# Norm chains without GpSimd, and a layer's modulation by TensorE instead of VectorE

## The chip, the cores and the metric

The kernel runs on one core of a Trainium2 chip. A core has five engines with queues of their own: TensorE (PE, matrix products), VectorE (DVE, elementwise work on two operands), ScalarE (ACT, functions and copies), GpSimd (POOL, elementwise work) and SyncE (SP, which here issues the DMAs). Each engine works through its queue in order and waits at semaphores for the others. The metric is the device time of one execution, in microseconds; smaller is better.

## The reference

A residual stream `x` of 512 tokens by 1024 features, and a context `xc` of 256 tokens, go through two blocks in fp32.

The first block has two layers. In each, a vector `c` gives six modulation vectors (shift, scale and gate for the mixer, and the same for the MLP), and `c_ctx` gives six for the context:

```python
sh1, sc1, g1, sh2, sc2, g2 = modulation(c, w_mod[l], b_mod[l])        # silu(c) @ w_mod + b_mod
csh1, csc1, cg1, csh2, csc2, cg2 = modulation(c_ctx, w_mod[l], b_mod[l])
px = modulate(rms_norm(x, norm1_g[l]), sh1, sc1) @ w_in[l]            # h * (1 + scale) + shift
...                                                                   # latent attention, Fourier mix, long convolution
x = x + g1 * heads_out(att_x, px, hy, w_out[l])
x = x + g2 * sq_relu_mlp(modulate(rms_norm(x, norm2_g[l]), sh2, sc2), w_mlp1[l], w_mlp2[l])
...                                                                   # in the first layer, the same for xc
```

A last `rms_norm` ends the block. The second block has two layers as well, with a norm on each sublayer's output too:

```python
u = rms_norm_2(h, norm_g[layer, 0]) * (1.0 + sc1) + sh1
y = hgrn2_mixer(u, ...)                      # layer 0; layer 1: dilated_attention_mixer
h = h + (1.0 + g1) * rms_norm_2(y, norm_g[layer, 1])
u = rms_norm_2(h, norm_g[layer, 2]) * (1.0 + sc2) + sh2
y = swiglu_ffn(u, ffn_w_in[layer], ffn_w_out[layer])
h = h + (1.0 + g2) * rms_norm_2(y, norm_g[layer, 3])
```

`rms_norm` divides by the root of the mean square over the 1024 features.

## The kernel before

Features lie on partitions: `x` is eight tiles of 128 features by 512 tokens. fp32 products are made of three products of split operands: every operand has a high part (a rounded cast by ACT) and a low part (the rest, one subtraction of two SBUF tiles). `mm3` (L153 to L155) issues high x high, high x low and low x high.

**Weights.** `wchunk` fetches a chunk of 128x1024 by a DMA from SP into `wr` (three buffers); ACT casts it to `w_h` (L118), and POOL subtracts to make `w_l` (L119). In some stretches there is a second ring of five buffers, `wx_h` and `wx_l` (`extra_ring`), so that the first eight chunks of a product (its head) are resident while two halves of the tokens pass. `gemm` goes over the chunks `m`; with `parts` the head is gone through once for each half of the tokens, so that the second half's norm runs beside the first half's products.

**Norms.** A norm over features is a chain. ACT squares a tile and DVE (or POOL, for the second half) adds it to the sum (`stat_add`, L284; `st_h` for 256 tokens, `st_f` for 512). A product with a matrix of ones (L307) sums over partitions; ACT and DVE make the reciprocal root `st_rh` (L316, L317). Then each tile is scaled (`md_h`, L326), and split into `u_h` and `u_l` (`modulate`, L335, L336): every third tile goes a second way, where ACT works twice and POOL subtracts (L333). In the second block a sublayer's output `y` is normed first: DVE makes `r_t` (L1292), adds it to `x` (L1293) and the squares of the new `x` are added for the next norm. `final_norm` (L1266) does the like between the blocks. These chains stand in a list, `self.chain`; `gemm` calls `link` after each chunk, which issues up to three steps of it. So they run beside the products of the other half.

The four places where the output of one part is normed, added and normed again are: the first block's end and the HGRN2 layer's start, that layer's output projection and its FFN's start, that FFN's end and the dilated attention's start, and that layer's output projection and its FFN's start.

**Modulation vectors.** They are products of one row with a large matrix. `mod_tasks` makes them on DVE: a piece of weights 128x512 (256 KB) comes into `mo_w`, and DVE multiplies it by a column of `c` and adds it to `mo_a` (L378 for the first of eight pieces, L380 for the others; for the first layer a second time with `c_ctx`). After eight pieces PE transposes `mo_a` (L363), and DVE reduces it over the 128 partial sums. The pieces are tasks in a list, `self.bgq`; `gemm` calls `bg(3)` after each chunk in w_in and w_out, which issues three of them. `run_late` puts the last step of a set behind the next chunk's products.

A scheduler then places each engine's instructions in its queue, by its own estimate of when their inputs are ready; so the order in a queue is not the order of the code.

Of the kernel before, what the change touches and what calls it, by code (L numbers as in the profile page):

```python
# [14 lines left out]
ALU = mybir.AluOpType  # L15
# [3 lines left out]
P = 128  # L19
D = 1024  # L20
KD = D // P
# [58 lines left out]
class Kern:  # L80
# [60 lines left out]
    def wchunk(self, src, n=1024, parts=P, extra=False, lo_eng=None):  # L141

        nc = self.nc
        raw = self.t(self.ring, [P, 1024], "wr", 3)
        nc.sync.dma_start(raw[:parts, :n], src)
        w = self.hl(self.xring, [P, 1024], "wx", 5) if extra else self.hl(self.ring, [P, 1024], "w", 3)
        w = w[:parts, :n]
        self.split(w, raw[:parts, :n], lo_eng or nc.gpsimd)
        return w
# [21 lines left out]
    def gemm(self, srcs, nk, rhs, segs, evac, head=2, parts=None, after=None, n=1024, bg=0, lead=2, dep=False):  # L171
# [11 lines left out]
        parts = [(x,) for x in parts] if parts else [seg(0)]  # L183
        short = self.xring is None and parts[-1][-1][1] - parts[-1][0][0] <= C
        load = lambda m, short=False: self.wchunk(
            srcs[m], n, extra=self.xring is not None and m > 2, lo_eng=self.nc.vector if short and m % 3 == 2 else None)
        head = min(head, len(srcs))
        keep = [load(m) for m in range(head)] if self.xring is not None else None
        for part in parts if head else ():
# [30 lines left out]
    @contextmanager  # L220
    def extra_ring(self, side="right"):
        with self.pool("xring", side) as p:
            self.xring = p
            yield
            self.xring = None
# [121 lines left out]
    def mod_tasks(self, pool, wkey, bcol, pairs, js, pad=0):  # L347
# [6 lines left out]
        for j in js:  # L354
            use = [pr for pr in pairs if j in pr[2]]
            for half in range(2):
# [29 lines left out]
                for k in range(KD):  # L386
                    tasks.append(lambda k=k, f=piece: f(k))
                tasks += [lambda: None] * pad
        return tasks

# [445 lines left out]
    def block1_layer(self, l):  # L836
# [56 lines left out]
        if not last:  # L893
            fl, self.bgq = self.bgq, self.mod_tasks(
                hvp, "w_mod0", self.bmod[0],
                [(self.c1, self.m1[0], range(2, 6)), (self.cc, self.mc[0], range(2, 6))], range(2, 4), pad=1)
            for i, step in enumerate(fl):
                self.bgq.insert(3 * i + 3 * (i > 0), step)
            win(0, 8, tok, evac_hyena, parts=SEGS)
            wes.close()  # L900
            mid = lay.enter_context(self.pool("mid"))
# [117 lines left out]
        if not last:  # L1019
# [9 lines left out]
            for k in range(4):  # L1029
# [3 lines left out]
            p = tmp.enter_context(self.pool("mods", "right"))  # L1033
            self.bgq += self.mod_tasks(
                p, "w_mod0", self.bmod[0],
                [(self.c1, self.m1[0], range(4, 5)), (self.cc, self.mc[0], range(4, 5))], range(4, 5), pad=1)

# [75 lines left out]
    def norm_to(self, pool, key, st, g, m, j, s, e, lag=0):  # L1113
# [7 lines left out]
        def tile(k):  # L1121
            o = j * KD + k
            self.modulate(pool, self.xk(k, s, e), v["r"], v["g"][:, k : k + 1], m[:, o : o + 1], self.u[k][:, s:e],
                          k % 3 == 2)

# [129 lines left out]
    def final_norm(self, s, e):  # L1255
# [8 lines left out]
        def tile(k):  # L1264
            x = self.xk(k, s, e)
            nc.vector.scalar_tensor_tensor(x, x, self.fin_g[:, k : k + 1], v["r"], op0=ALU.mult, op1=ALU.mult)  # L1266
            self.stat_add(self.stp, self.st[s], x, nc.gpsimd if s else None)

# [6 lines left out]
    def resid2(self, l, j, p, y, sty, s, e):  # L1275
# [13 lines left out]
        def tile(k):  # L1289
# [4 lines left out]
            if not last:  # L1294
                self.stat_add(self.stp, self.st[s], x, nc.gpsimd if s else None)
            elif k % 2:
# [23 lines left out]
    def hgrn(self, es_x):  # L1320
# [7 lines left out]
        with ExitStack() as es:  # L1328
# [9 lines left out]

            ws = [[self.wchunk(a["hg_wv"][c, kp], extra=4 * c + kp > 2) for kp in range(4)] for c in range(2)]
            for s, e in HALVES:  # L1340
# [200 lines left out]
    def dilated(self, es_x):  # L1541
        with ExitStack() as es:
            cp = es.enter_context(self.pool("cat"))
            cat = [self.hl(cp, [P, L], f"cat{k}") for k in range(KD)]
            with ExitStack() as hs:
                p = hs.enter_context(self.pool("qk"))
                self.dilated_heads(p, hs, es_x, cat)
            es_x.enter_context(self.extra_ring())
            with self.pool("y") as yp:
# [458 lines left out]
```

## Time and profile before

| | |
|---|---|
| median of 3 runs | 3566.88 us (3566.8 to 3569.93) |
| profiled execution | 3567.03 us |
| its span | 3565.2 us |
| PE busy | 3305.0 us, 93% |
| DVE busy | 2122.9 us, 60% |
| ACT busy | 1296.0 us, 36% |
| POOL busy | 1378.7 us, 39% |
| mean granted clock of PE | 0.969 |

The span runs from the first instruction to the last. An engine's busy time is that in which it executes; what it waited for is told by the table of waits, which names the engine, tile and line that released it. PE's granted clock is a share of full speed. Since only one engine is near its limit over the whole span, the stretches have to be looked at one by one.

### The profile page before, as it was taken

Reading aid. Unit: us, or ns where it says so; the run is one execution under the profiler, and the core shown is the slowest. Engines: PE = TensorE matmul, PEld = TensorE weight load, DVE = VectorE, ACT = ScalarE, POOL = GpSimd, SP = SyncE. Lnnn points to the kernel's source line nnn. Section 1 sums busy time; section 2 is a strip of 40 time slices with the busy share of each in tenths; the row PEclk is TensorE's granted clock in tenths of the full one; section 3 lists DMA queues with packets and bytes.
Section 4 is the critical chain, followed back from the end, with each engine's and each line's share of the span. In section 5 each row is a group of like instructions: output and inputs, shape, how many; then the busy total and the mean of one; then the engine's idle time right before and its main releaser. Section 6 shows DMA issues by size and latency. Waiting matters only on the chain. (4 is left out here: it accounts for less than half of the span.)

```text
span 3565.2 us, 46665 instructions
## 1 busy us (share of the span) xinstructions
PE 3305.0 (93%) x18232; PEld 2779.7 (78%) x18232; DVE 2122.9 (60%) x3144; ACT 1296.0 (36%) x2278; POOL 1378.7 (39%) x730
## 2 busy tenths in 40 slices
PE   7988988999998988999989898999899999989998
PEld 3776667888886766988877787888788878888887
DVE  7677778575466467757674656476585474461224
ACT  4235634121124346422245555222323323352222
POOL 2424434232234344434443344344433333434443
PEclk9989999999999999999999999999999999989999
DMA  6330044343343210345531123455313223322332
GB/s 207 122 98 26 24 136 122 119 123 122 122 127 95 95 45 30 110 136 188 184 122 57 56 85 93 150 183 186 101 52 101 92 75 100 102 65 89 95 95 71
DMA packets 145344, 374.31 MB, mean 105 GB/s; under 512 B 19515, under 2 KB 28770, under 8 KB 145124
## 3 DMA queue, kind: packets, MB, share of 16 engines
q1 hardware_dynamic: 140900, 367.14, 32.6%
q10 hardware_dynamic: 4224, 4.19, 0.3%
q8 instruction: 143, 2.34, 0.3%
q14 instruction: 77, 0.63, 0.1%
HBM read 364.98 MB, written 6.29 MB: 104 GB/s over the span
## 5 line engine op out<-in xcount | busy, mean ns | idle before, releaser
L119 POOL TENSOR_TENSOR w_l<-wr,w_h 128x1024 fp32r<-128x1024 f32 (+1 forms) x401 | 967.4, 2414 | 1642.5 <-ACT w_h L118 1592.6
L153 PE MATMUL A<-u_h,w_h 128*128 128x512 f32 (+1 forms) x2344 | 879.2, 376 | 12.8 <-ACT w_h L118 3.7
L154 PE MATMUL A<-u_l,w_h 128*128 128x512 f32 (+1 forms) x2344 | 874.9, 373 | 8.0 <-DVE u_l L336 5.5
L155 PE MATMUL A<-u_h,w_l 128*128 128x512 f32 (+1 forms) x2344 | 873.6, 373 | 8.3 <-POOL w_l L119 8.3
L118 ACT CAST w_h<-wr 128x1024 fp32r<-128x1024 f32 (+1 forms) x406 | 420.3, 1037 | 1085.2 <-PE A L154 725.9
L153 PEld LDWEIGHTS A<-u_h,w_h 128*128 128x128 f32 x2344 | 450.3, 192 | 103.4 <-ACT w_h L118 5.8
L155 PEld LDWEIGHTS A<-u_h,w_l 128*128 128x128 f32 x2344 | 450.9, 192 | 91.9 <-POOL w_l L119 10.0
L154 PEld LDWEIGHTS A<-u_l,w_h 128*128 128x128 f32 x2344 | 450.6, 192 | 91.1 <-DVE u_l L336 6.7
L380 DVE SCALAR_TENSOR_TENSOR mo_a<-mo_w,mc_c,mo_a 128x512 f32<-128x512 f32 x308 | 323.4, 1050 | 105.2 <-DMA mo_w<-in_ada_dram 59.4
L155 PE MATMUL A<-hid_h,w_l 128*128 128x512 f32 (+1 forms) x1072 | 376.9, 352 | 8.4 <-POOL w_l L119 8.4
L154 PE MATMUL A<-hid_l,w_h 128*128 128x512 f32 (+1 forms) x1072 | 378.6, 353 | 3.5 <-DVE hid_l L119 3.5
L153 PE MATMUL A<-hid_h,w_h 128*128 128x512 f32 (+1 forms) x1072 | 379.2, 354 | 1.9 <-ACT hid_h L118 1.9
L155 PEld LDWEIGHTS A<-hid_h,w_l 128*128 128x128 f32 x1072 | 203.4, 190 | 38.4 <-POOL w_l L119 10.5
L154 PEld LDWEIGHTS A<-hid_l,w_h 128*128 128x128 f32 x1072 | 203.8, 190 | 31.5 <-DVE hid_l L119 4.7
L153 PEld LDWEIGHTS A<-hid_h,w_h 128*128 128x128 f32 x1072 | 203.5, 190 | 30.1 <-ACT hid_h L118 2.9
L1751 DVE TENSOR_TENSOR sg<-A,sg 128x512 f32<-128x512 f32 (+1 forms) x52 | 31.4, 608 | 242.6 <-PE A L155 209.0
L119 POOL TENSOR_TENSOR wx_l<-wr,wx_h 128x1024 fp32r<-128x1024 f32 x55 | 134.4, 2457 | 79.4 <-ACT wx_h L118 74.7
L1134 DVE SCALAR_TENSOR_TENSOR x<-A,m,x 128x512 f32<-128x512 f32 (+1 forms) x96 | 62.0, 657 | 169.7 <-PE A L155 169.7
L284 DVE TENSOR_TENSOR st_h<-st_h,st_sh 128x256 f32<-128x256 f32 x137 | 108.6, 800 | 56.6 <-ACT st_sh L283 52.6
L1081 DVE TENSOR_TENSOR relu<-relu 128x512 f32<-128x512 f32 (+1 forms) x104 | 83.7, 833 | 82.5 <-ACT relu L1080 82.3
L1583 DVE TENSOR_TENSOR qk<-A,cos 128x512 f32<-128x512 f32 (+1 forms) x56 | 47.0, 841 | 131.0 <-PE A L155 130.8
L153 PE MATMUL A<-w_h,u_h 128*128 128x256 f32 (+1 forms) x408 | 120.7, 296 | 2.1 <-DVE rt L1586 2.1
(553 smaller groups left out, 6264.4 us busy)
## 6 DMA issues: line engine op xcount, KB each, us to landing
wr<-in_w_mlp_dram SPq DMA_DIRECT2D x139, 512.0 KB, 3.7
mo_w<-in_ada_dram SPq DMA_DIRECT2D x192, 256.0 KB, 3.5
wr<-in_ff_win_dram SPq DMA_DIRECT2D x88, 512.0 KB, 3.6
mo_w<-in_w_mod_dram SPq DMA_DIRECT2D x160, 256.0 KB, 3.1
wr<-in_at_wqk_dram SPq DMA_DIRECT2D x48, 512.0 KB, 3.6
wr<-in_ff_wout_dram SPq DMA_DIRECT2D x32, 512.0 KB, 3.6
wr<-in_w_in_dram SPq DMA_DIRECT2D x30, 512.0 KB, 3.6
wr<-in_w_out_dram SPq DMA_DIRECT2D x24, 512.0 KB, 3.6
```

Of the source, the lines that this page charges most:

```text
L118: nc.scalar.copy(dst.hi, src)
L119: (lo_eng or nc.vector).tensor_tensor(dst.lo, src, dst.hi.bitcast(F32), op=ALU.subtract)
L153: ins = mm(out, lhs.hi, rhs.hi, start=first, stop=False)
L154: mm(out, lhs.hi, rhs.lo, start=False, stop=False)
L155: mm(out, lhs.lo, rhs.hi, start=False, stop=last)
L284: (eng or nc.vector).tensor_tensor(acc, acc, sq, op=ALU.add)
L380: nc.vector.scalar_tensor_tensor(state[i], raw, cc[:, k : k + 1], state[i], op0=ALU.mult, op1=ALU.add)
L1081: nc.vector.tensor_tensor(r, r, r, op=ALU.mult)
L1134: nc.vector.scalar_tensor_tensor(x, ps, mod[:, o : o + 1], x, op0=ALU.mult, op1=ALU.add)
L1583: nc.vector.tensor_tensor(d, vw(ps), vw(c), op=ALU.mult)
L1751: nc.vector.tensor_tensor(sgs[s], ps, sgs[s], op=ALU.mult)
```

## The change

Five things change.

1. The low halves of weights in products that wait for a norm (`dep`: the first eight chunks or fewer of the MLPs, of the dilated attention's q and k, and of the FFNs), and those of the HGRN2 layer's first eight chunks, are made by DVE instead of POOL: 46 subtractions of 128x1024. Where there is a second ring, its chunks 3, 4 and 5 are loaded first.
2. The second ring has six buffers instead of five after the dilated attention.
3. `modulate` no longer sends every third tile of a norm over POOL; DVE makes all `u_l`.
4. The adds of squares of the second half in `final_norm` and `resid2` move from POOL to DVE: 28 of 128x256.
5. For the first layer, the mixer's gate and the MLP's shift and scale (for `c` and for `c_ctx`) are made by `mod_products` instead of `mod_tasks`. In twelve quarters of 256 outputs each, one DMA brings 128x8x256 weights (1 MB, a single buffer), and eight fp32 products use them as the moving operand; the stationary one, `c32`, has 32 columns, of which `c` and `c_ctx` are the first two and the rest zero. The eight products go to four column groups of PE, two after each other on each. ACT copies the 128x256 result out of PSUM, PE transposes it (two transposes), and DVE adds up the four groups. A quarter is five tasks: the load, three empty ones, the products.

```diff
         load = lambda m, short=False: self.wchunk(
-            srcs[m], n, extra=self.xring is not None and m > 2, lo_eng=self.nc.vector if short and m % 3 == 2 else None)
+            srcs[m], n, extra=self.xring is not None and m > 2,
+            lo_eng=self.nc.vector if dep or short and m % 3 == 2 else None)
         head = min(head, len(srcs))
-        keep = [load(m) for m in range(head)] if self.xring is not None else None
+        keep = None
+        if self.xring is not None:
+
+            order = sorted(range(head), key=lambda m: (m not in (3, 4, 5), m)) if dep else range(head)
+            keep = {m: load(m) for m in order}
...
+    def mod_products(self, pool, wkey, bcol, pairs, js, gap, rows_in):
...
+        c32 = self.t(pool, [P, KD, 32], "mp_c")
+        nc.gpsimd.memset(c32, 0.0)
+        nc.gpsimd.tensor_copy(c32[:, :, 0], self.c1)
+        nc.gpsimd.tensor_copy(c32[:, :, 1], self.cc)
+        for j in js:
+            for quarter in range(4):
+                state = {}
+
+                def load(j=j, quarter=quarter, state=state):
+                    self.run_late()
+                    half, c = divmod(quarter, 2)
+                    state["w"] = raw = self.t(pool, [P, KD, 256], "mp_w")
+                    nc.sync.dma_start(raw, self.a[wkey][j * 2 + half].rearrange("k p n -> p k n")[:, :, c * 256 : c * 256 + 256])
+
+                def products(j=j, quarter=quarter, state=state):
+                    ps = self.psa()[:, :256]
+                    for k in range(KD):
+                        g = 32 * (k % 4)
+                        nc.tensor.matmul(ps[g : g + 32], c32[:, k], state["w"][:, k], start=k < 4, stop=k >= 4,
+                                         tile_position=(0, g))
+                    state["a"] = self.t(rows_in[0], [P, 512], rows_in[1])[:, :256]
+                    nc.scalar.copy(state["a"], ps)
+                    self.late.append(lambda: finish(j * KD + quarter * 2, state["a"]))
+
+                def finish(o, rows):
+                    ps = self.psa()[:, :256]
+                    for m in range(2):
+                        nc.tensor.transpose(ps[:, m * P : (m + 1) * P], rows[:, m * P : (m + 1) * P], self.ident)
+                    sums = ps.rearrange("p (m g c) -> p m g c", g=4, c=32)
+                    for i, out in enumerate(pairs):
+                        nc.vector.reduce_sum(out[:, o : o + 2], sums[:, :, :, i], axis=AX.X)
+                        nc.vector.tensor_tensor(out[:, o : o + 2], out[:, o : o + 2], bcol[:, o : o + 2], op=ALU.add)
+
+                tasks += [load] + [lambda: None] * gap + [products]
+        return tasks
...
-            fl, self.bgq = self.bgq, self.mod_tasks(
-                hvp, "w_mod0", self.bmod[0],
-                [(self.c1, self.m1[0], range(2, 6)), (self.cc, self.mc[0], range(2, 6))], range(2, 4), pad=1)
+            fl, self.bgq = self.bgq, self.mod_products(hvp, "w_mod0", self.bmod[0], (self.m1[0], self.mc[0]), range(2, 4), 3,
+                                                    (hvp, "mp_a"))
...
-            self.bgq += self.mod_tasks(
-                p, "w_mod0", self.bmod[0],
-                [(self.c1, self.m1[0], range(4, 5)), (self.cc, self.mc[0], range(4, 5))], range(4, 5), pad=1)
+            self.bgq += self.mod_products(p, "w_mod0", self.bmod[0], (self.m1[0], self.mc[0]), range(4, 5), 3,
+                                          (self.stp, "st_r"))
...
-            self.modulate(pool, self.xk(k, s, e), v["r"], v["g"][:, k : k + 1], m[:, o : o + 1], self.u[k][:, s:e],
-                          k % 3 == 2)
+            self.modulate(pool, self.xk(k, s, e), v["r"], v["g"][:, k : k + 1], m[:, o : o + 1], self.u[k][:, s:e])
...
-            self.stat_add(self.stp, self.st[s], x, nc.gpsimd if s else None)
+            self.stat_add(self.stp, self.st[s], x)
...
-                self.stat_add(self.stp, self.st[s], x, nc.gpsimd if s else None)
+                self.stat_add(self.stp, self.st[s], x)
...
-            ws = [[self.wchunk(a["hg_wv"][c, kp], extra=4 * c + kp > 2) for kp in range(4)] for c in range(2)]
+            ws = [[self.wchunk(a["hg_wv"][c, kp], extra=4 * c + kp > 2, lo_eng=nc.vector) for kp in range(4)] for c in range(2)]
...
-            es_x.enter_context(self.extra_ring())
+            es_x.enter_context(self.extra_ring(6))
```

In the new file the lines named above stand seven lower, those from 1134 on 48 lower (L284 is L291, L1292 is L1340).

On DVE, after the HGRN2 layer's output projection, the order before, from the last steps of the first half's residual to that half's reciprocal root (`st_rh_18254`):

```order
L1292 SCALAR_TENSOR_TENSOR r_t_18188<-y_17769,gain_3407_18087,st_rh_18080 128x256
L284 TENSOR_TENSOR st_h_18089<-st_h_18089,st_sh_18179 128x256
L1293 TENSOR_TENSOR x_3881<-x_3881,r_t_18188 128x256
L284 TENSOR_TENSOR st_h_18089<-st_h_18089,st_sh_18185 128x256
L284 TENSOR_TENSOR st_h_18089<-st_h_18089,st_sh_18191 128x256
L284 TENSOR_TENSOR st_h_18074<-st_h_18074,st_sh_18220 128x256
L284 TENSOR_TENSOR st_h_18074<-st_h_18074,st_sh_18249 128x256
L316 SCALAR_TENSOR_TENSOR st_sh_18257<-B_18252,st_sh_18257 128x256
L284 TENSOR_TENSOR st_h_18074<-st_h_18074,st_sh_18297 128x256
L317 SCALAR_TENSOR_TENSOR st_rh_18254<-st_sh_18257,st_rh_18254 128x256
```

The same place after (the reciprocal root is `st_rh_18198`; L119 with `w_l` or `wx_l` is a subtraction that makes low halves of weights):

```order
L1341 TENSOR_TENSOR x_3853<-x_3853,r_t_18132 128x256
L119 TENSOR_TENSOR wx_l_18394<-wr_18391,wx_h_18393 128x1024
L291 TENSOR_TENSOR st_h_18033<-st_h_18033,st_sh_18129 128x256
L119 TENSOR_TENSOR wx_l_18400<-wr_18397,wx_h_18399 128x1024
L291 TENSOR_TENSOR st_h_18033<-st_h_18033,st_sh_18135 128x256
L291 TENSOR_TENSOR st_h_18018<-st_h_18018,st_sh_18164 128x256
L291 TENSOR_TENSOR st_h_18018<-st_h_18018,st_sh_18193 128x256
L119 TENSOR_TENSOR wx_l_18406<-wr_18403,wx_h_18405 128x1024
L119 TENSOR_TENSOR w_l_18412<-wr_18409,w_h_18411 128x1024
L323 SCALAR_TENSOR_TENSOR st_sh_18201<-B_18196,st_sh_18201 128x256
L291 TENSOR_TENSOR st_h_18018<-st_h_18018,st_sh_18241 128x256
L324 SCALAR_TENSOR_TENSOR st_rh_18198<-st_sh_18201,st_rh_18198 128x256
```

Four weight subtractions have come to stand between the residual and the reciprocal root; before, all eight were in POOL's queue.

On PE, at the end of the first layer's w_in, the order before (L966 and L967 double the rows of a key tile `kk`, L363 transposes `mo_a`, L548 belongs to the convolution):

```order
L966 MATMUL A_1814<-kk_h_1810,dupr_1283 128x512
L967 MATMUL A_1814<-kk_l_1811,dupr_1283 128x512
L966 MATMUL A_1824<-kk_h_1820,dupr_1283 128x256
L363 MATMUL A_1836<-c_ident_67,mo_a_342_1634 128x128 x4
L967 MATMUL A_1824<-kk_l_1821,dupr_1283 128x256
L363 MATMUL A_1843<-c_ident_67,mo_a_343_1636 128x128 x4
L548 MATMUL A_1897<-c_ident_67,eo_400_1890 128x128 x4
```

The same place after (L424 are the products on column groups, whose weights `mp_w` are the moving operand, L433 the transposes of their copied results `mp_a`):

```order
L1016 MATMUL A_1770<-kk_h_1766,dupr_1267 128x512
L1017 MATMUL A_1770<-kk_l_1767,dupr_1267 128x512
L1016 MATMUL A_1780<-kk_h_1776,dupr_1267 128x256
L424 MATMUL A_1784<-mp_w_1706,mp_c_485 32x256 x2
L1017 MATMUL A_1780<-kk_l_1777,dupr_1267 128x256
L424 MATMUL A_1784<-mp_w_1706,mp_c_485 32x256 x6
L433 MATMUL A_1795<-c_ident_67,mp_a_1793 128x128 x2
L424 MATMUL A_1804<-mp_w_1802,mp_c_485 32x256 x8
L433 MATMUL A_1815<-c_ident_67,mp_a_1813 128x128 x2
L599 MATMUL A_1869<-c_ident_67,eo_385_1862 128x128 x4
```

Two quarters of products stand here one behind the other, each with its transposes right behind it, where two sets of transposes of `mo_a` were.

## Rows read from the trace of the kernel before

**Rows 1.** The page: busy us, share of the span, instructions of each engine.

```profile
PE 3305.0 (93%) x18232; PEld 2779.7 (78%) x18232; DVE 2122.9 (60%) x3144; ACT 1296.0 (36%) x2278; POOL 1378.7 (39%) x730
```

**Rows 2.** PE's waits, whole span: us in total, times, longest.

```profile
PE B L307 <- DVE st_h L284: 46.6, 9, 8.4
PE A L155 <- POOL w_l L119: 22.1, 14, 2.6
PE B L307 <- POOL st_h L284: 13.7, 3, 5.5
PE B L307 <- DVE st_f L284: 12.3, 5, 4.3
PE A L363 <- DVE mo_a L380: 11.6, 1, 11.6
...
PE A L966 <- ACT kk_h L118: 6.8, 4, 2.3
```

**Rows 3.** Stretches: us long, busy us of PE, PEld, DVE, ACT, POOL, clock, DMA share.

```profile
485.00:498.00 13.00, 1.36 (x7) 0.94 (x6) 10.69 (x12) 2.86 (x4) 4.68 (x2) 0.71 0.75 234
1833.00:1891.00 58.00, 46.19 (x255) 40.38 (x254) 45.62 (x68) 29.24 (x56) 27.48 (x17) 0.82 0.29 87
2146.00:2201.00 55.00, 39.05 (x281) 37.18 (x280) 41.39 (x67) 28.87 (x63) 27.36 (x17) 0.90 0.30 89
2171.00:2176.00 5.00, 5.00 (x24) 4.83 (x23) 2.96 (x6) 1.74 (x5) 2.38 (x1) 0.50 0.50 116
2558.00:2607.00 49.00, 33.02 (x228) 31.81 (x227) 45.64 (x77) 21.09 (x45) 24.28 (x17) 0.82 0.30 92
3137.00:3185.00 48.00, 33.63 (x241) 32.48 (x240) 39.59 (x64) 24.37 (x55) 25.06 (x16) 0.84 0.30 88
```

**Rows 4.** Timeline of DVE: start us, us, operation, count.

```profile
2152.41 3.02 DVE L1292 SCALAR_TENSOR_TENSOR r_t<-y,gain,st_rh 128x256 f32<-128x256 f32 x2
2155.35 2.94 DVE L1293 TENSOR_TENSOR x<-x,r_t 128x256 f32<-128x256 f32 x2
2158.22 0.87 DVE L1292 SCALAR_TENSOR_TENSOR r_t<-y,gain,st_rh 128x256 f32<-128x256 f32 x2
2159.01 0.74 DVE L1293 TENSOR_TENSOR x<-x,r_t 128x256 f32<-128x256 f32 x2
```

**Rows 5.** Timeline of POOL from 2146.

```profile
2152.47 5.21 POOL L119 TENSOR_TENSOR w_l<-wr,w_h 128x1024 fp32r<-128x1024 f32 x2 [1.91 <-ACT w_h L118]
```

**Rows 6.** Groups of DVE, 2146 to 2201: count, busy us, mean ns, idle before.

```profile
L1292 DVE SCALAR_TENSOR_TENSOR r_t<-y,gain,st_rh 128x256 f32<-128x256 f32 x16 | 12.8, 835 | 0.1
L1293 DVE TENSOR_TENSOR x<-x,r_t 128x256 f32<-128x256 f32 x16 | 9.3, 618 | 0.0
L284 DVE TENSOR_TENSOR st_h<-st_h,st_sh 128x256 f32<-128x256 f32 x14 | 8.1, 600 | 0.7 <-ACT st_sh L283 0.6
L336 DVE SCALAR_TENSOR_TENSOR u_l<-md_h,m,u_h 128x256 fp32r<-128x256 f32 x6 | 6.5, 1104 | 3.0 <-ACT u_h L335 2.9
```

**Rows 7.** Groups of POOL, 2146 to 2201.

```profile
L284 POOL TENSOR_TENSOR st_h<-st_h,st_sh 128x256 f32<-128x256 f32 x7 | 6.1, 868 | 6.7 <-ACT st_sh L283 6.4
```

**Rows 8.** DVE on the tile w_l: min, median, max ns, first and last start.

```profile
L119 DVE TENSOR_TENSOR w_l<-wr,w_h x5: 1208/1212/2594, 527.2 to 1112.7; 128x1024 fp32r<-128x1024 f32 x5
```

**Rows 9.** Timeline of all engines, end of the first layer's mixer.

```profile
492.67 2.40 DVE L284 TENSOR_TENSOR st_f<-st_f,st_sq 128x512 f32<-128x512 f32 x1 [0.74 <-ACT st_sq L283]
...
497.11 1.97 PE L363 MATMUL A<-c_ident,mo_a 128*128 128x128 f32 x8 [11.64 <-DVE mo_a L380]
```

**Rows 10.** Timeline of PE, three places.

```profile
40.31 5.50 PE L822 MATMUL B<-wr,c 128*2 128x512 f32 x12
...
212.91 1.04 PE L363 MATMUL A<-c_ident,mo_a 128*128 128x128 f32 x8
...
1952.11 2.37 PE L1452 MATMUL A<-st,qd 128*32 128x128 f32 x32
```

**Rows 11.** The page, DMA issues: count, KB each, median us to landing.

```profile
wr<-in_w_mlp_dram SPq DMA_DIRECT2D x139, 512.0 KB, 3.7
```

More of the change, by code (lines that the diff above doesn't have):

```diff
@@ L145, in wchunk @@
         nc.sync.dma_start(raw[:parts, :n], src)
-        w = self.hl(self.xring, [P, 1024], "wx", 5) if extra else self.hl(self.ring, [P, 1024], "w", 3)
+        w = self.hl(self.xring, [P, 1024], "wx", self.xbufs) if extra else self.hl(self.ring, [P, 1024], "w", 3)
         w = w[:parts, :n]
@@ L220, in extra_ring @@
     @contextmanager
-    def extra_ring(self, side="right"):
+    def extra_ring(self, bufs=5, side="right"):
+        self.xbufs = bufs
         with self.pool("xring", side) as p:
@@ L388, in mod_tasks @@
                 tasks += [lambda: None] * pad
+        return tasks
+    def mod_products(self, pool, wkey, bcol, pairs, js, gap, rows_in):
+        nc = self.nc
+        tasks = []
+        c32 = self.t(pool, [P, KD, 32], "mp_c")
[28 more added lines that the diff above has]
+                tasks += [load] + [lambda: None] * gap + [products]
         return tasks
```

## The prediction

> **What bounds the kernel now.** I read the engine table first: TensorE (PE) is busy for 93% of the span [rows 1], so time can come only from its gaps, its clock, or its work. The table of PE's waits over the whole span is next [rows 2]. Its largest rows are not weights that arrive late but norms: the ones-matmul that sums squares (L307) waits for adds of squares, 46.6 us for VectorE (DVE) adds, 13.7 for GpSimd (POOL) adds, 12.3 for the 512-wide adds of the first block. One wait of 11.6 us is for the modulation sums (mo_a) that DVE makes, and 22.1 us in 14 waits are for low halves of weights that POOL makes.
>
> Third, the table of stretches [rows 3] shows where the norm waits lie: four places in which one sublayer's output is normed, added and normed again (1833 to 1891, 2146 to 2201, 2558 to 2607, 3137 to 3185). There DVE is busy for 41.4 of 55 us, 45.6 of 49, 39.6 of 48 and 45.6 of 58, and PE's granted clock is 0.82 to 0.90. DVE with its chain, not PE, sets the end of these stretches.
>
> Fourth, DVE's timeline at 2152 shows why [rows 4]: two r_t operations of 128x256 take 3.02 us, two adds to x 2.94; three microseconds later the same pairs take 0.87 and 0.74. In the first pair's time POOL runs two weight splits (L119), 5.21 us without a break [rows 5]. The stretched operations read two SBUF tiles each. So an operation of DVE with two SBUF inputs loses up to 1.5 us when it meets a POOL split.
>
> **The norm chains.** Take 2146 to 2201. The grouped rows [rows 6] give r_t 12.8 us (16), x 9.3 (16), the adds 8.1 (14), u_l 6.5 (6): 36.7 us. At the undisturbed pace of rows 4 (0.44 for r_t and, as the same kind, u_l; 0.37 for x and, as the same kind and size, the adds) they would take 16 x 0.44 + 16 x 0.37 + 14 x 0.37 + 6 x 0.44 = 20.7. So 16.0 us of DVE's time there are collisions. What comes to DVE in exchange: eight splits at 1.21, the median of the five that DVE makes today [rows 8], 9.7 us; POOL's seven adds, now 0.868 us each [rows 7], 7 x 0.37 = 2.6; two u_l, 0.9. Together 13.2. DVE's load falls by only 2.8 us.
>
> The gain is larger than that only if the splits fit where DVE sits idle, 55 - 41.4 = 13.6 us, most of it while a statistic goes through PE and ScalarE (ACT). DVE's new order puts four of the eight splits ahead of the first half's rstd, where it waits for adds and the statistic, three among that half's u tiles, and the last behind the second half's rstd, ahead of its r_t. If half of the 9.7 us falls into idle time, the stretch ends 2.8 + 4.9 = 7.7 us earlier; with all in it 12.5, with none of it 2.8, and if each split also holds up a link of the chain (eight times 1.21, nothing hidden) the stretch loses up to 7. I take 7, since the tail also loses POOL's slower adds. The stretch at 3137 has 8.4 us of idle time and the same operations: 7. The one at 2558 has only 3.4 us idle: 5. The one at 1833 has 12.4 but its chain also waits for PE's results on their way to x: 6. Together -25, and between +28 (four times 7) and -42 (12.5, 12.5, 2.8 + 8.4 and 2.8 + 3.4).
>
> By the Trainium skill, "SBUF — State Buffer", section "Who interferes with whom", a DVE instruction with two SBUF inputs contends with a GpSimd instruction that reads SBUF, and the loser is blocked for the other's whole length. The trace agrees (0.44 against 1.5 us each). By that rule a split on DVE is itself such an instruction, and would be blocked wherever POOL still works; the five of today reach from 1.21 to 2.59 us [rows 8], and at the far end eight would cost 11 us more in a stretch.
>
> **The other splits and tiles.** Fourteen more splits go to DVE, six at the first layer's MLP and eight at the second's. A share of the 22.1 us of waits for w_l [rows 2] lies at the end of the first layer's mixer and the start of its MLP; I take 4 us of gain there, 1 at the second layer, and 2 for the u_l tiles that no longer go over ACT twice and POOL. Sum -7; between +5 (DVE has no free time there either) and -14. The sixth buffer and the order in which head chunks are loaded I cost at nothing: transfers of 512 KB land in 3.7 us [rows 11], and the DMA share of those stretches is 0.29 to 0.30 [rows 3].
>
> **The modulation of the first layer.** Removed: 96 DVE operations, which costs PE nothing except where it waited. It did at 485: mo_a was late by 11.64 us, with an add of 2.40 us in its chain that met POOL [rows 9]. The 8.4 us wait of rows 2 ends at 2170; from 2171 to 2176 the granted clock was 0.50, 1.2 instead of 2.4 GHz [rows 3], which is 2.5 us of work lost; I take the same here. Of the 12.3 us of waits for 512-wide adds [rows 2], which share DVE's queue with such sums, I take 4. Gain 11.6 + 2.5 + 4 = 18.
>
> Added, all on PE: twelve quarters of eight products with 32x256 results. No row shows this shape. Sixteen fp32 matmuls of 32x128 on four column groups take 2.37 us (32 records, two each) [rows 10], 0.148 each: by number of matmuls a quarter costs 1.2 us, by columns 2.4. Plain fp32 on 512 columns costs 5.50 / 12 = 0.46 a record, two records each [rows 10], so 0.46 for 256 columns and 3.7 a quarter. Twelve quarters: 14, 28 or 44 us. I take 21, between the two readings of the nearest row, as that row can't tell overhead from columns. The transposes fall from six sets of eight at 1.04 us [rows 10] to twelve pairs, 6.2 to 3.1 us: -3.
>
> By the Trainium skill, "TensorEngine Tiling (Array Packing)", section "When to Use Tiling", a free dimension of 32 gives four-fold column tiling. With that the plain price would fall to 11 us, and the sum by 10; the row of L1452 doesn't show so much.
>
> Then waits. In PE's new order most pairs of transposes stand right behind their products, so PE waits for ACT's copy of the result: four waits for an ACT cast of k cost 6.8 us, 1.7 each [rows 2], as the upper end; I take half of it, 0.8, as the copy is a single operation of 256 columns, for eight of them: 6 us. At the end of w_in the eighth quarter's products come right behind the seventh's transposes, while their 1 MB load can start only when the seventh's products have left the single buffer. 512 KB land in 3.7 us [rows 11], so 1 MB takes some 6, and PE waits with nothing else in front of it: 6, and 1 for the clock. Added 21 - 3 + 6 + 7 = 31. Net +13; between -7 (14 for products, waits hidden in gaps that PE has there anyway) and +67 (44 for products, copies at 1.7 = 14, and a wait of 6 at five of the loads = 30, less 3 and 18).
>
> **Sum.** The profiled execution took 3567.03 us (span 3565.2 and 1.8 outside it), 0.15 above the median of the runs. 3567 - 25 - 7 + 13 = 3548 us.
>
> **Rivals.** (1) The splits fall into DVE's idle time, -42, the products overlap and their waits lie in gaps, -7: 3567 - 42 - 7 - 7 = 3511; halfway to it 3530. For it: DVE idles 38 us in the four stretches. Against it: the idle time comes where a statistic isn't ready, and a split can only use it if ACT's cast of that chunk is done by then.
> (2) DVE becomes the bound of the stretches: the splits stand in its queue ahead of links of the chain, as the order shows for four of them, and the price cancels the gain; 3567 + 0 - 7 + 13 = 3573. For it: DVE's load falls by a mere 2.8 of 41.4 us.
> (3) Slower: the products of the first layer. From the point where their added PE time and waits pass 18 + 32 = 50 us, the whole change loses; at their upper end 3567 - 32 + 67 = 3602. For it: PE has no free time in w_in, the load has one buffer, and at 485 the DMA share is already 0.75 [rows 3]. Against it: five stalls of 6 us each would be needed as well as no overlap of column groups.
>
> **How the numbers follow.** A measurement of this kernel tells 0.2%, 7 us, from no change: faster is under 3560, slower above 3574. The forecast, 3530 to 3560 around 3548, gets 0.50; rival 1, 3505 to 3530, 0.25; rival 2, 3560 to 3574, 0.14; rival 3 0.11. The range that leaves some 0.2 out runs from 3516 to 3575. Faster 0.75, same 0.14, slower 0.11.
>
> **What would show it.** In the four stretches: r_t at about 0.44 us and x at 0.37 with no long ones, the longest wait of L307 (8.4 us) cut to a few microseconds, and the stretch 5 to 9 us shorter; no PE wait for a split of DVE. In w_in: products at 1.2 to 2.4 us a quarter, transposes that wait about 0.8 us for ACT, one wait of about 6 us for a load. At the end of the first mixer: the 11.6 us gap gone and no wait for the loads in its place. The forecast is wrong if splits on DVE take over 2 us in the mean, if r_t stays long, if PE waits for weights in a stretch, or if products take 3.7 us a quarter.

## The result and the profile after

The changed kernel takes 3508.74 us (median of 4 runs, 3505.51 to 3513.84), 0.984 of the kernel before (95% interval 0.9822 to 0.9858): 58 us faster by the medians, where 19 were forecast, and below the range. Differences in the experiments below are worked out from such ratios and the 3566.8 us of the kernel before.

The engine table of the changed kernel:

```profile
PE 3287.6 (94%) x18400; PEld 2757.6 (79%) x18400; DVE 2013.0 (57%) x3173; ACT 1288.1 (37%) x2260; POOL 1212.6 (35%) x635
```

Beside rows 1, VectorE has lost 110 us of busy time, GpSimd 166, PE 17. PE's waits over the whole span, as in rows 2:

```profile
PE B L314 <- DVE st_h L291: 20.1, 7, 6.5
...
PE A L155 <- DVE w_l L119: 10.1, 4, 4.7
...
PE A L155 <- POOL w_l L119: 9.9, 8, 1.9
...
PE A L424 <- DMA mp_w<-in_w_mod_dram: 8.9, 2, 4.7
...
PE B L314 <- DVE st_f L291: 4.2, 3, 2.1
...
PE A L433 <- ACT st_r L427: 3.5, 4, 1.0
...
PE A L433 <- ACT mp_a L427: 3.2, 5, 0.9
```

The norm waits (L314, before L307) fell from 46.6 and 13.7 us to 20.1, those for 512-wide adds on this tile from 12.3 to 4.2, and the 11.6 us wait for mo_a is gone. New are waits for the 1 MB loads (8.9), for ACT's copies ahead of the transposes (3.5 and 3.2) and for splits on DVE (10.1). Of these 10.1 us, 6.2 lie in the third of the four stretches:

```profile
PE A L155 <- DVE w_l L119: 6.2, 2, 4.7
```

The cleanest measure of the four stretches is the time from the first to the last of their four statistics, the ones-matmuls. First the table of these stretches before (us long, busy us of PE, PEld, DVE, ACT, POOL, clock, DMA share):

```profile
1833.56:1890.77 57.21, 45.40 (x249) 39.62 (x247) 45.62 (x68) 29.24 (x56) 27.48 (x17) 0.82 0.30 88
2146.96:2200.49 53.53, 37.59 (x272) 35.72 (x270) 41.23 (x66) 28.36 (x62) 27.36 (x17) 0.90 0.30 89
2552.43:2606.56 54.13, 38.15 (x273) 36.89 (x271) 46.57 (x79) 25.89 (x52) 27.50 (x18) 0.84 0.29 86
3133.01:3184.82 51.81, 37.45 (x273) 36.23 (x271) 40.48 (x66) 27.56 (x61) 27.47 (x17) 0.86 0.28 82
sum 216.68, PE 158.58 PEld 148.46 DVE 173.89 ACT 111.05 POOL 109.81; mean PE 39.64 PEld 37.12 DVE 43.47 ACT 27.76 POOL 27.45
```

And after:

```profile
1828.05:1867.47 39.42, 38.67 (x248) 34.69 (x247) 37.09 (x82) 24.31 (x49) 0.00 (x0) 1.00 0.40 128
2123.42:2166.01 42.59, 34.20 (x272) 32.90 (x270) 36.89 (x83) 27.72 (x59) 0.00 (x0) 0.97 0.34 106
2516.17:2557.66 41.49, 33.09 (x250) 31.72 (x249) 38.33 (x91) 24.39 (x49) 0.53 (x1) 0.92 0.22 73
3085.80:3124.21 38.41, 33.88 (x272) 32.83 (x270) 35.90 (x82) 25.06 (x57) 0.00 (x0) 0.98 0.31 97
sum 161.91, PE 139.85 PEld 132.15 DVE 148.21 ACT 101.47 POOL 0.53; mean PE 34.96 PEld 33.04 DVE 37.05 ACT 25.37 POOL 0.13
```

They shrank from 216.7 to 161.9 us together, by 54.8: nearly all of the gain is here. DVE's busy time in them fell by 25.7 us although it now makes splits; its idle time fell from 42.8 (216.7 less 173.9) to 13.7. The clock, 0.82 to 0.90 before, is 0.92 to 1.00, and POOL is all but silent.

DVE's timeline at the place of rows 4, and its groups there, show what a collision had cost:

```profile
2127.91 0.88 DVE L1340 SCALAR_TENSOR_TENSOR r_t<-y,gain,st_rh 128x256 f32<-128x256 f32 x2
2128.71 0.76 DVE L1341 TENSOR_TENSOR x<-x,r_t 128x256 f32<-128x256 f32 x2
...
2136.12 1.21 DVE L119 TENSOR_TENSOR wx_l<-wr,wx_h 128x1024 fp32r<-128x1024 f32 x1
2137.26 0.41 DVE L291 TENSOR_TENSOR st_h<-st_h,st_sh 128x256 f32<-128x256 f32 x1
2137.59 1.21 DVE L119 TENSOR_TENSOR wx_l<-wr,wx_h 128x1024 fp32r<-128x1024 f32 x1
```

```profile
L291 DVE TENSOR_TENSOR st_h<-st_h,st_sh 128x256 f32<-128x256 f32 x21 | 8.6, 421 | 0.4 <-ACT st_sh L290 0.2
L1340 DVE SCALAR_TENSOR_TENSOR r_t<-y,gain,st_rh 128x256 f32<-128x256 f32 x16 | 7.2, 485 | 0.0
L1341 DVE TENSOR_TENSOR x<-x,r_t 128x256 f32<-128x256 f32 x16 | 6.2, 424 | 0.0
L119 DVE TENSOR_TENSOR wx_l<-wr,wx_h 128x1024 fp32r<-128x1024 f32 x5 | 6.1, 1219 | 0.0
...
L343 DVE SCALAR_TENSOR_TENSOR u_l<-md_h,m,u_h 128x256 fp32r<-128x256 f32 x8 | 3.5, 484 | 0.7 <-ACT u_h L342 0.7
```

The first r_t pair takes 0.88 us instead of 3.02, the adds to x 0.76 instead of 2.94; the means beside rows 6 are 485 instead of 835 ns, 424 instead of 618, 421 instead of 600, 484 instead of 1104. A split on DVE takes 1.22 us, and stands between the adds (2136 to 2139).

The 3.02 us of the first pair before are not two operations of 1.5 us. The first took 0.49 us; the second ran beside a split on POOL, and as long:

```profile
2152.81 2.62 DVE L1292 SCALAR_TENSOR_TENSOR r_t<-y,gain,st_rh 128x256 f32<-128x256 f32 x1
2152.47 2.68 POOL L119 TENSOR_TENSOR w_l<-wr,w_h 128x1024 fp32r<-128x1024 f32 x1 [1.91 <-ACT w_h L118]
```

In the four stretches before, 25 operations of DVE took 2.0 to 2.7 us, each of them beside one of the 32 splits on POOL; after, none takes longer than a split, 1.23.

### The profile page after: what moved, and what is told of

It is laid out like the page before. It is cut to its first block, busy times and chain, and to the rows that moved or that the text cites. A ratio compares the mean times of both kernels' runs of the same rounds, so it can differ in the third digit from the quotient of the medians.

```text
span 3504.3 us, 46813 instructions
## 1 busy us (share of the span) xinstructions
PE 3287.6 (94%) x18400; PEld 2757.6 (79%) x18400; DVE 2013.0 (57%) x3173; ACT 1288.1 (37%) x2260; POOL 1212.6 (35%) x635
## 3 DMA queue, kind: packets, MB, share of 16 engines
q10 hardware_dynamic: 4224, 4.19, 0.4%
## 5 line engine op out<-in xcount | busy, mean ns | idle before, releaser
L119 POOL TENSOR_TENSOR w_l<-wr,w_h 128x1024 fp32r<-128x1024 f32 (+1 forms) x381 | 915.2, 2404 | 1900.7 <-ACT w_h L118 1891.3
L387 DVE SCALAR_TENSOR_TENSOR mo_a<-mo_w,mc_c,mo_a 128x512 f32<-128x512 f32 x266 | 278.4, 1047 | 81.0 <-DMA mo_w<-in_ada_dram 53.4
L154 PE MATMUL A<-w_l,u_h 128*128 128x256 f32 (+1 forms) x408 | 119.8, 294 | 0.0
L155 PE MATMUL A<-w_h,u_l 128*128 128x256 f32 (+1 forms) x408 | 118.8, 291 | 0.0
```

Of the source, the lines that this page charges most:

```text
L119: (lo_eng or nc.vector).tensor_tensor(dst.lo, src, dst.hi.bitcast(F32), op=ALU.subtract)
L154: mm(out, lhs.hi, rhs.lo, start=False, stop=False)
L155: mm(out, lhs.lo, rhs.hi, start=False, stop=last)
L387: nc.vector.scalar_tensor_tensor(state[i], raw, cc[:, k : k + 1], state[i], op0=ALU.mult, op1=ALU.add)
```

## Experiments

**The two halves apart.** The fifth edit alone (the loads, splits, tiles and adds of edits one to four put back), shown at two of its places:

```diff
-            lo_eng=self.nc.vector if dep or short and m % 3 == 2 else None)
+            lo_eng=self.nc.vector if short and m % 3 == 2 else None)
...
-            self.stat_add(self.stp, self.st[s], x)
+            self.stat_add(self.stp, self.st[s], x, nc.gpsimd if s else None)
```

> The kernel before with the fifth edit alone: the first layer's mixer gate and MLP shift and scale by products on column groups. By the sum of the prediction this part costs 13 us: 3580. By a comparison of the two traces (both reach the first attention's keys at 289 us, and the mixer's output projection then takes 63.8 instead of 67.2 us) it gains about 3: 3564. If the part were worth 10 us or more by itself, the norm chains would have given that much less: 3556 or below.

Measured: 0.9988 (0.9979 to 0.9997), 4 us faster. Then edits one to four alone, with `mod_tasks` called as before:

> The changed kernel with the modulation put back on VectorE: edits one to four alone. By the sum of the prediction they gain 32 us: 3535. By the two traces the four stretches gain 56 us together (19.3, 10.7, 12.9 and 13.4) and the rest little: 3510 to 3514. If the edits need each other (the modulation frees VectorE for splits in the first layer) this and the run of the fifth edit alone add up to clearly less than the whole, 58 us.

Measured: 0.9844 (0.983 to 0.9858), 56 us faster. The halves add up to 60; they don't need each other. The prediction's 13 us of cost for the modulation and its 32 us for the rest were both wrong, to the same side.

**Splits or adds.** The first edit without its loading order, on the kernel before:

```diff
-            srcs[m], n, extra=self.xring is not None and m > 2, lo_eng=self.nc.vector if short and m % 3 == 2 else None)
+            srcs[m], n, extra=self.xring is not None and m > 2, lo_eng=self.nc.vector if dep or short and m % 3 == 2 else None)
...
-            ws = [[self.wchunk(a["hg_wv"][c, kp], extra=4 * c + kp > 2) for kp in range(4)] for c in range(2)]
+            ws = [[self.wchunk(a["hg_wv"][c, kp], extra=4 * c + kp > 2, lo_eng=nc.vector) for kp in range(4)] for c in range(2)]
```

> The kernel before with the first edit's move alone: 46 subtractions of weights from GpSimd to VectorE, in the old loading order, the adds of squares and every third tile still on GpSimd. If collisions with the 2.4 us splits are what stretches the chains, this alone brings most of it: 35 to 45 us, 3522 to 3532. If GpSimd's slow adds at the tail and the tiles that go over it are what counts, it gains less than 15 us: over 3552.

Measured: 0.9861 (0.9846 to 0.9875), 50 us faster, by its middle above even the upper end. And the third and fourth edit alone (no `k % 3 == 2`, no `nc.gpsimd if s else None`):

> The kernel before with the third and fourth edit alone: the adds of the second half and all low halves of normed tiles on VectorE, the weight splits still on GpSimd. By the collision theory VectorE then has more operations that meet GpSimd's splits, so little is won: 0 to 12 us, 3555 to 3567. If the adds and tiles are what counts, 30 us or more: below 3537.

Measured: 0.9991 (0.998 to 1.0002), 3 us and not told from nothing. The splits' move carries the change. Beside it, the adds and tiles with the ring and the loading order bring 6 us by the middle of intervals that overlap (0.9844 against 0.9861), which doesn't tell them from nothing.

**What a split costs, on POOL and on DVE.** The low halves of 40 chunks left out:

```diff
+        if lo_eng == "none":
+            nc.scalar.copy(w.hi, raw[:parts, :n])
+            return HL(w.hi, w.hi)
```

On the changed kernel:

> The changed kernel without the 40 weight subtractions that it makes on VectorE in the second layer's MLP and the four stretches (the products there read the high half twice, so the low halves of these chunks are left out). It tells what the splits cost where they now are, 40 x 1.22 = 49 us of VectorE. If they stand on the path as the prediction had it for half of them: 20 to 25 us faster than the changed kernel, 3484 to 3489. If they fall into VectorE's idle time: within 8 us of it, 3501 to 3509.

Measured: 0.9806 (0.9793 to 0.982), 12 us faster than the changed kernel: about half of what the prediction had on the path. On the kernel before:

> The kernel before without the low halves of the 40 chunks of the second layer's MLP and the four stretches (their products read the high half twice), the adds of squares and every third tile still on GpSimd. It tells what the splits cost where they were, on GpSimd. The prediction had 12.5 us a stretch at most, some 45 in all: 3520. The four stretches of the run without low halves on the changed kernel were 65 us shorter between the first and the last of their statistics than before; if the splits on GpSimd are nearly all of that, 55 to 65 us: 3500 to 3510. If the slow adds on GpSimd held a good part of it, 45 or less: over 3520.

Measured: 0.9834 (0.982 to 0.9847), 59 us faster. So on POOL these splits cost 59 us, though PE hardly waited for them: without them its waits for low halves that POOL makes are 20.6 us, where they were 22.1 [rows 2].

```profile
PE A L158 <- POOL w_l L119: 20.6, 14, 2.4
```

On DVE, whose time they take, they cost 12. The sums of the same stretches, without the low halves, in the kernel before and in the changed one:

```profile
sum 156.78, PE 140.07 PEld 133.25 DVE 119.08 ACT 107.89 POOL 33.13; mean PE 35.02 PEld 33.31 DVE 29.77 ACT 26.97 POOL 8.28
```

```profile
sum 151.78, PE 139.63 PEld 133.27 DVE 119.38 ACT 105.23 POOL 0.53; mean PE 34.91 PEld 33.32 DVE 29.85 ACT 26.31 POOL 0.13
```

Against 216.7 and 173.9 before, taking the splits off POOL removes 54.8 us of DVE's busy time and 59.9 of the stretches: the first figure is what the collisions took. Against the second sum, the splits on DVE add 28.8 us of busy time (148.2 less 119.4) and 10.1 us to the stretches: two thirds lie in idle time. If that reading holds, the idle time is used up, and the same work once more must cost far more:

```diff
+        if lo_eng == "twice":
+            nc.vector.tensor_tensor(w.lo, raw[:parts, :n], w.hi.bitcast(F32), op=ALU.subtract)
```

> The changed kernel with each of the 40 subtractions on VectorE made twice (same result, 49 us more of VectorE). The first 49 us cost 16. If they were cheap because VectorE idled while a statistic went through PE and ScalarE, that idle time is now used up and the second 49 us cost clearly more, 30 to 49: 3539 to 3558. If they were cheap because the chain doesn't end the stretches, the second cost as little as the first, 10 to 20: 3519 to 3529.

Measured: 0.9935 (0.992 to 0.9949), 34 us slower than the changed kernel; the first 49 us of subtractions cost 12, the second 34. (The 16 in the expectation is a difference of medians that were taken apart; by the ratios it is 12.) The sum of the four stretches with the subtractions made twice:

```profile
sum 177.18, PE 136.38 PEld 127.67 DVE 166.82 ACT 103.08 POOL 0.53; mean PE 34.09 PEld 31.92 DVE 41.70 ACT 25.77 POOL 0.13
```

DVE's busy time there is 18.6 us more than in the changed kernel and the stretches are 15.3 us longer, so only 3.3 us went into idle time, where 18.7 of the first 28.8 had. That fits idle time that is used up. But it isn't the chain alone: weights come late too.

```profile
PE A L155 <- ACT w_h L118: 19.4, 7, 6.7
PE A L157 <- DVE w_l L150: 11.9, 2, 7.4
```

PE waits 19.4 us for casts of weights, 3.3 in the changed kernel, and 4.5 and 7.4 us for low halves that DVE makes late. How much of the 34 us each of the two took, no run tells.

**The clock.** PE's busy time in the four stretches fell, with a higher clock. To see whether that is a cause, products of constants were put into the waits of the kernel before:

```diff
+        for _ in range(warm):
+            nc.tensor.matmul(ps[:, :P], self.ones, self.ones, start=True, stop=True)
         nc.tensor.matmul(ps, self.ones, acc, start=True, stop=True)
```

> The kernel before with products of two constant matrices (128x128, 5 to 32 of them) put ahead of the ones-matmul of the four norms where PE waited 4 to 8 us, into the PSUM tile that it then overwrites. They change nothing but what PE does in the wait. If 20 of the 56 us of the stretches are work that PE did at the lower clock after such waits, this gains 10 to 20 us with the waits of DVE unchanged: 3547 to 3557. If the longer matmuls after a wait have another cause, or the stretch's end is set by VectorE all along, nothing is won or the products cost: 3565 to 3575.

Measured: 1.0027 (1.0016 to 1.0038), 10 us slower. The clock did rise: at the place where the table of stretches has 0.50 [rows 3], this kernel has 0.72. The second of the four stretches and the five microseconds behind its wait, the sum of the four stretches, and the timeline of PE at the wait:

```profile
2145.36:2199.19 53.83, 41.53 (x334) 40.71 (x332) 41.00 (x66) 29.03 (x62) 27.43 (x17) 0.97 0.29 91
2170.00:2175.00 5.00, 5.00 (x33) 5.00 (x33) 3.30 (x8) 2.95 (x8) 0.00 (x0) 0.72 0.24 93
```

```profile
sum 217.06, PE 177.25 PEld 169.78 DVE 171.35 ACT 112.29 POOL 110.65; mean PE 44.31 PEld 42.45 DVE 42.84 ACT 28.07 POOL 27.66
```

```profile
2157.29 7.30 PE L311 MATMUL B<-ones 128*128 128x128 f32 x64
2168.90 0.82 PE L312 MATMUL B<-st_h,ones 128*128 128x256 f32 x2 [4.31 <-DVE st_h L287]
```

But the stretch takes 53.8 us, as before (53.5), and the four together 217.1 (216.7): faster products only reach the next statistic earlier, and wait there for DVE. The lower clock there followed from DVE's delay, and raising it gained nothing. What makes the kernel 10 us slower outside the four stretches isn't shown. On the changed kernel:

> The changed kernel with 20 and 14 such products ahead of the two longest waits that are left in its second-block norms (5.9 us and 4.0 us). By the clock theory 2 to 6 us faster, 3503 to 3507; by the rival no change or up to 3 us slower.

Measured: 0.9842 (0.9828 to 0.9855), the same. No run shows a gain from the clock in these stretches.

**The first layer's splits.** Left on POOL where there is no second ring (`dep and self.xring is not None`):

> The changed kernel with the six splits of the first layer's MLP back on GpSimd. In its trace PE waits 6.2 us for VectorE's residual of the context and 3.4 us for a split on VectorE just there (540 to 551), where before it waited 2.4 and 2.6 us for GpSimd's splits. If the splits delay VectorE there, this gains 2 to 6 us: 3503 to 3507. If the waits come from the products and transposes ahead of them, nothing: 3507 to 3511.

Measured: 0.9857 (0.9844 to 0.9871), 6 us slower by the middle of intervals that just overlap. The rows I had blamed stayed: in this kernel, too, PE waits 6.2 us for the context's residual and 3.4 for a split on DVE, one that DVE made before the change as well.

```profile
PE A L153 <- DVE xc L1182: 6.2, 1, 6.2
PE A L155 <- DVE w_l L119: 3.4, 1, 3.4
```

The prediction had 4 us for these six; the run doesn't contradict it, and can't confirm it.

**What the modulation costs in each form.** The pieces or the products left out, their vectors a constant (one of two places; the call in the mixer's output projection goes too):

```diff
-            fl, self.bgq = self.bgq, self.mod_tasks(...)
+            fl, self.bgq = self.bgq, []
+            for mm in (self.m1[0], self.mc[0]):
+                nc.gpsimd.memset(mm[:, 2 * KD : 5 * KD], 0.25)
```

> The kernel before without the modulation's 96 pieces, which the fifth edit replaces (the first layer's mixer gate and MLP shift and scale are set to a constant). It tells what these pieces cost in all. The prediction had 18 us: 3547. But the fifth edit gained 4 us though it brought some 40 us of products, transposes and waits, so they should cost about 45 us: 3515 to 3525.

Measured: 0.9957 (0.9944 to 0.9969), 15 us. The prediction's 18 was for the waits and the clock alone; this run also lacks the six sets of transposes, 6 in its sum, so it should have shown 24. My later 45 was further off.

> The changed kernel without the twelve quarters of products (the same vectors set to a constant). It tells what the products cost in all. The prediction had 31 us: 3477. The rows of the changed kernel add up to 23 us of products, 8 of transposes, 7 of waits for ACT's copy and 9 for two loads, 47, of which some lies in waits that PE has there anyway: 3462 to 3475. If most of it is hidden, 3490 or more.

Measured: 0.9805 (0.9791 to 0.9819), 12 us less than the changed kernel, where the prediction had 31 net of the old transposes, 37 with them. The 47 in the expectation is wrong: it took 1.93 us, the eighth quarter, for every quarter, and 0.69, its transposes, for every pair. That quarter ran at a granted clock of 0.50, the lower of the two levels (1.2 GHz), right behind a wait. The fourth quarter ran at 1.00 (the table shows it and then the eighth, the timeline the fourth):

```profile
175.22:176.29 1.07, 1.07 (x17) 0.42 (x16) 0.10 (x1) 1.07 (x3) 0.00 (x0) 1.00 0.00 0
244.24:246.17 1.93, 1.93 (x16) 0.59 (x16) 0.00 (x0) 0.00 (x0) 0.00 (x0) 0.50 0.00 0
```

```profile
175.22 1.07 PE L424 MATMUL A<-mp_w,mp_c 128*32 128x256 f32 x16
177.11 0.44 PE L433 MATMUL A<-c_ident,mp_a 128*128 128x128 f32 x2 [0.82 <-ACT mp_a L427]
```

Nine of the twelve quarters take 1.07 us, and three, at 0.50, take 1.93 to 2.99: 16.5 in all. The pairs of transposes take 0.38 to 0.44 us at 1.00 and 0.69 at 0.50, 5.8 in all. With 6.7 of waits for ACT's copy and 8.9 for two loads the rows add up to 38 us. The table of w_in, from its first product to the first attention's keys, and of the mixer's output projection, of the kernel without the products and of the changed one:

```profile
61.40:286.90 225.50, 201.54 (x956) 157.58 (x957) 108.12 (x169) 78.17 (x143) 84.01 (x62) 0.89 0.22 70
459.00:515.10 56.10, 50.07 (x238) 40.93 (x236) 23.85 (x24) 16.28 (x23) 20.64 (x8) 1.00 0.41 131
```

```profile
63.15:289.82 226.67, 205.07 (x1100) 158.68 (x1101) 108.97 (x201) 79.83 (x150) 85.44 (x66) 0.93 0.32 103
462.68:526.50 63.82, 55.16 (x290) 42.35 (x288) 24.73 (x42) 16.26 (x26) 17.85 (x7) 0.95 0.52 175
```

In w_in, 144 more records of PE make the stretch 1.2 us longer; in the mixer's output projection 52 more make it 7.7 us longer. In w_in the kernel without them waits instead, and its clock is 0.89 instead of 0.93:

```profile
PE A L540 <- DVE fo L535: 10.4, 3, 5.4
```

It waits 10.4 us for the convolution's filters from DVE, a wait that the changed kernel doesn't have. I had taken PE's 93% for a stretch without room.

**Room at the end of w_in.** One number, `range(2, 4), 3,` to `range(2, 4), 2,`:

> The changed kernel with two empty tasks between a quarter's load and its products in w_in instead of three, so that all eight quarters fit between the chunks and none is left over at the end. If the 4.2 us wait for the last load and the products behind it are a cost of their own, 3 to 7 us faster: 3502 to 3506. If the next wait (the convolution's first inputs from VectorE) takes its place, the same: 3507 to 3511.

Measured: 0.9818 (0.9805 to 0.983), 3501.67 us, 8 us faster than the changed kernel and 65 faster than the one before. The two intervals overlap by a little, the runs (3499.80 to 3502.18 against 3505.51 to 3513.84) do not. The changed kernel's timeline at the end of w_in, where the eighth quarter stands right behind the seventh:

```profile
238.93 0.38 SPq L418 DMA_DIRECT2D mp_w<-in_w_mod_dram  x1
...
239.36 0.69 PE L433 MATMUL A<-c_ident,mp_a 128*128 128x128 f32 x2 [0.47 <-ACT mp_a L427]
...
244.24 1.93 PE L424 MATMUL A<-mp_w,mp_c 128*32 128x256 f32 x16 [4.19 <-DMA mp_w<-in_w_mod_dram]
...
246.72 0.69 PE L433 MATMUL A<-c_ident,mp_a 128*128 128x128 f32 x2 [0.55 <-ACT mp_a L427]
```

Its load is issued when the seventh products are done, and PE waits 4.19 us for it and runs the eighth at the lower clock. With a gap of two the last quarter is between chunks, no wait for a load is left in w_in, and all eight quarters take 1.07 us. The stretch of w_in is 218.5 us instead of 226.7:

```profile
64.60:283.10 218.50, 202.05 (x1101) 158.42 (x1102) 110.05 (x201) 78.30 (x149) 85.53 (x62) 0.95 0.33 107
```

**Buffers and order.** Five buffers, chunks in natural order:

> The changed kernel with five buffers in the second ring throughout and the head's chunks loaded in their natural order. The prediction costs both at nothing: 3506 to 3512. If a sixth buffer and the early load of the chunks 3 to 5 are what keeps the weights ahead of the products, 5 us or more slower: over 3513.

Measured: 0.9833 (0.9821 to 0.9846): the same.

## Why the prediction was wrong

*The place and the mechanism were right.* Four stretches, DVE's chain as their end, stretched by POOL's splits, and splits that cost half the time on DVE: the rows after show each, and the splits' move alone brings 50 of 58 us. The undisturbed paces (0.44, 0.37, 1.21) came out at 0.485, 0.42 and 1.22. One reading was off: a collision doesn't cost an operation "up to 1.5 us", which is the mean of a pair. One of the two took 0.49 us, the other 2.62, some 2.2 more than alone. The sum used the groups' means and isn't touched by it.

*The step that failed first is the sum of a stretch*, "the stretch ends 2.8 + 4.9 = 7.7 us earlier", and the -25 for four. Its parts, over four stretches, from the sums above: the collisions were put at 16.0 less the 3.5 of added adds and tiles, 12.5 each, 50 in all; without splits on either engine DVE's busy time is 54.5 lower, so this was nearly right. Half of the splits' 39 us was put on the path, 19; 10 were. And DVE's idle time was held constant except for what splits fill; it fell by another 10 us without any split (42.8 to 32.4; 37.7 with the splits gone and the adds and tiles still on POOL). A chain that waits in turn for DVE, PE and ACT may get shorter in all its links; no run tests that by itself. Then the text took less than its own working (7, 5, 6 and 7 instead of 7.7 each), for reasons that the runs do not bear out; the one at 1833 gave 17.8. So: 50 - 19 - 6 became 25, where 54.5 + 10.4 - 10.1 = 54.8 was measured. The upper bound of 42 failed for the same reason: it had no term for idle time that goes away.

*The second is "Added 21 - 3 + 6 + 7 = 31"* for the products. The rows came out near it: twelve quarters take 16.5 us (21 forecast; at full clock 1.07 each, a little under the reading "by number of matmuls"), the transposes 5.8 (3.1), waits for ACT's copies 6.7 (6), and two late loads 8.9 (one of 6, and 1 for the clock): 38 where 37 were forecast, before the 6 of the old transposes. What failed is the step from rows to time: these 38 us cost 12, as PE had waits in w_in that they filled. The gain side, 18 and those 6, measured 15. The sum, +13, should have been -3, and alone it measured -4.

*Rivals.* Rival 1 was the case, and the time went a little beyond its 3511. Rival 2 (DVE's queue as the new bound) and rival 3 (the products) are out: PE's waits for norms fell in each stretch (in the second from 12.9 to 6.2 us), and no quarter took 3.7 us. One sign that was to tell against the forecast came true all the same: in the third stretch PE waits 6.2 us for two low halves that DVE makes late.

By the Trainium skill ("SBUF — State Buffer", section "Who interferes with whom"), a DVE instruction with two SBUF inputs contends with a GpSimd instruction that reads SBUF. The rows agree: 0.88 us a pair where POOL is silent, 3.02 where it ran, and the operation that was held took 2.62 us beside a split of 2.68. That splits on DVE would be blocked in turn had no occasion, since POOL does next to nothing in these stretches any more.

By the Trainium skill ("TensorEngine Tiling (Array Packing)", section "When to Use Tiling"), a free dimension of 32 gives four-fold column tiling. The rows come near it: a quarter's 1.07 us at a granted clock of 1.00 is 3.4 times less than the 3.7 of plain fp32, worked out from the row of L822, which ran at 1.00 too.

## What to carry to other kernels

Price a helper engine's work by what it does to the engine that sets the end, not by who waits for it: 40 splits on an engine that is 39% busy cost 59 us, and 12 on the one whose chain they had stretched. When a chain alternates between engines, count its idle links too: they shrink with it, and they hide new work until they are full. Here the same work then cost three times as much, part of it because weights came late. Rows of PE are not time: 38 us of them cost 12 where PE had waits of its own, and a higher clock gave nothing where another engine ended the stretch. And before a row becomes a price, look at the granted clock beside it: a quarter right behind a wait took 1.93 us, nine of the twelve 1.07.

## What the runs showed of the hardware

An operation of DVE with two SBUF inputs that ran beside a subtraction on POOL took as long as that one (2.62 us beside 2.68, 0.47 alone). Products of constants in a wait kept the granted clock up (0.72 where it had been 0.50 in the microseconds behind the wait) without any gain in time. Column groups of 32 took fp32 products of 32x256 at 0.134 us each, 1.07 us for eight, at a granted clock of 1.00, and 1.93 for eight at 0.50. The row of L1452 has 0.148 us each for 128 columns at 1.00, so twice the columns didn't cost more. The first product of w_in started between 56.7 and 68.3 us in the profiled executions, also of kernels that are alike up to there, so single profiles can't settle a few microseconds.
